# Order of three weight splits, the first gather and a conditional block in the expert stage of a fused block kernel

## The chip, the cores and the metric

The kernel runs on one core of one Trainium2 chip. The metric is device time of one execution in microseconds (us). Three runs of the kernel before took 2264.12, 2265.87 and 2269.25 us; their median is 2265.87 us. Clock rows give TensorE's granted clock as a share of its full speed.

## The reference

The reference computes two transformer-like blocks on 512 tokens of width 1024 in float32. The stage that is changed here is the mixture of experts in the middle of the first block. Cut to what matters:

```python
logits = xt @ w_router + b_router                 # 512 tokens, 32 experts
top_vals, top_idx = lax.top_k(logits, 4)          # four experts a token
weights = jax.nn.softmax(top_vals, axis=-1)
# for each expert, on the tokens that chose it:
gu = xblk @ w_gu[e] + b_gu[e]                     # 1024 -> 2048
gate, up = jnp.split(gu, 2, axis=-1)
gate = jnp.minimum(gate, 7.0)
up = jnp.clip(up, -7.0, 7.0)
act = (up + 1.0) * gate * jax.nn.sigmoid(1.702 * gate)
y[token] += weight * (act @ w_down[e] + b_down[e])   # 1024 -> 1024
```

Every expert's weights are read once: 8 MB of w_gu and 4 MB of w_down in float32. Before this stage stand a modulated norm, a gated linear attention with pooling and the router; after it a second block with Fourier mixing, attention and a recurrent layer.

## The kernel before, in words

The program is written with a planner: the code traces instructions, and a planner with a cost model of its own puts them into one fixed order for each engine. Trace order is the priority; an instruction that the model holds to be ready sooner may be put ahead of one traced earlier. `tc.issue_after(ins)` adds one constraint: what the block traces on the engine of `ins` stands behind `ins` in that engine's order. On the chip each engine then works through its own list in order and waits at semaphores.

**Precision.** Each float32 weight block is split into two parts, `whi` (the rounded part, a cast on ACT, L147) and `wlo` (the rest, a subtraction on DVE, L148), by `split`. Products are the sum of three matmuls: whi with xTh, wlo with xTh, whi with xTl.

**Weights.** `Weights.get` takes the next raw block of [128, 2048] words (1 MB). Nine raw buffers rotate; SP issues the load of a block when the split of the block nine earlier has released its buffer. Four pairs of whi and wlo rotate as well (`pair`); a split can start when TensorE has finished with the block four earlier.

**One expert** (96 slots for its tokens) is `gate_up(e)`: 8 blocks of w_gu, for each 3 x 4 matmuls into `pgu` (four PSUM banks, one buffer), then four bias matmuls (L1139); `swiglu(e)`: on DVE g (L1166) and u (L1168) read pgu, on ACT the Silu (L1167), on DVE u times g (L1169); `down(e - 1)`: two bias matmuls, then 4 blocks of w_down (called d0, d2, d4 and d6 here, after k0), for each 2 x 3 x 2 matmuls into `pd` (L1183), then y on DVE (L1186) and a scatter with addition on POOL (L1187); `turn`: transposes of the activation (`paT`, they need u) into aTh and aTl. So TensorE's stream is gate_up(e), then down(e - 1) while DVE and ACT make the activation of e, and so on for 32 experts. In gate_up the transposes of the next expert's gathered tokens (`pxT`) stand at block 5, and for every fourth expert up to 24 the tables of the next four experts (`tables`) at block 1. In expert 6 there is extra work on DVE (`vectors`).

**The start.** The normed tokens go to DRAM (`h2d`, POOL's queue). Seven blocks of w_gu have been loaded by SP; blocks 7 and 8 are put on POOL's queue right behind the last h2d write (L1201); then POOL issues the gather of expert 0's tokens (L1119). `overflows` counts the blocks beyond 96 slots into a register of every engine (L995). `overflow` is a branch (L1007): if there are further blocks, a loop computes them; with these inputs it is jumped over. In trace order it stands ahead of the first three splits of expert 0 (`held`) and of `tables(0)`. It also takes one pair of the four (`ow`).

**The end.** The scatter of expert 31 must land before the next stage (`phase_c`) reads ydr back (hr, L1750). Meanwhile phase_c prepares spectra (pG) and its first weights.

Of the kernel before, what the change touches and what calls it, by code (L numbers as in the profile page):

```python
# [9 lines left out]
F32 = mybir.dt.float32  # L10
# [5 lines left out]
OP = mybir.AluOpType  # L16
# [4 lines left out]
D = 1024  # L21
# [5 lines left out]
NE = 32  # L27
TK, XK, BK = 1, 5, 4

AH, SH, HN = 9, 7, 3  # L30
# [76 lines left out]
def bcast(ap, n, off=0, parts=128):  # L107

    return bass.AP(tensor=ap.tensor, offset=ap.offset + off, ap=[[0, parts], [1, n]])
# [33 lines left out]
def split(S, hi, lo, src):  # L143
    if S.any:
        S.nc.any.tensor_copy(hi, src)
    else:
        S.nc.scalar.copy(hi, src)  # L147
    S.nc.vector.tensor_tensor(lo, src, hi.bitcast(F32), op=OP.subtract)  # L148


def mm3(S, ps, lh, ll, rh, rl, start, stop):
# [6 lines left out]
class Weights:  # L158
# [45 lines left out]
    def get(self, view, shape):  # L204
        S = self.S
        rv = self.early.pop(0) if self.early else self.load(view, shape)
        n = int(np.prod(shape[1:]))
        hi, lo = self.pair()
        hv, lv = hi[:shape[0], :n], lo[:shape[0], :n]
        if len(shape) == 3:  # L210
            hv = hv.rearrange("p (a b) -> p a b", a=shape[1])
            lv = lv.rearrange("p (a b) -> p a b", a=shape[1])
        split(S, hv, lv, rv)
        return hv, lv
# [742 lines left out]
def tables(S, pl, bank, b):  # L957

    nc = S.nc
    es = slice(b * 4, b * 4 + 4)  # L960
    oh = pl.tile([128, NT, 4, SLOTS], BF, name="oh", tag="oh", bufs=1)
    iota = S.k[:, None, K_IOTA:K_IOTA + SLOTS].to_broadcast([128, 4, SLOTS])
    for i in range(NT):
        nc.vector.tensor_tensor(oh[:, i], iota, S.pos[:, i, es, None].to_broadcast([128, 4, SLOTS]), op=OP.is_equal)
    p = bank("ptab")
    for e in range(4):
        for i in range(NT):
            nc.tensor.matmul(p[:SLOTS, e * 6:e * 6 + 6], oh[:, i, e, :], S.V[:, i, b * 4 + e, :], start=i == 0, stop=i == NT - 1)
    sl = pl.tile([SLOTS, 4, 6], F32, name="sl", tag="sl", bufs=2)
    nc.vector.tensor_copy(sl, p[:SLOTS, 0:24].rearrange("p (e c) -> p e c", e=4))  # L970
    t = pl.tile([SLOTS, 4, 4], F32, name="tsl", tag="tsl", bufs=2)
    tok, sct = t[:, :, 0], t[:, :, 1]
    nc.vector.tensor_tensor(tok, sl[:, :, 0], sl[:, :, 1], op=OP.add)
    nc.vector.tensor_copy(S.gi[:, es], tok)

    nc.vector.scalar_tensor_tensor(sct, sl[:, :, 2], S.k[:SLOTS, K_NSLOT:K_NSLOT + 1], tok, op0=OP.mult, op1=OP.add)
    nc.vector.tensor_scalar(S.si[:, es], sct, S.k[:SLOTS, K_SLOT:K_SLOT + 1], None, op0=OP.add)
    nc.vector.tensor_tensor(sct, sl[:, :, 3], sl[:, :, 4], op=OP.add)
    nc.vector.tensor_tensor(S.wt[:, es], sct, sl[:, :, 5], op=OP.add)
# [114 lines left out]
def phase_b(S):  # L1094
    nc, tc, I = S.nc, S.tc, S.I
    mm = nc.tensor.matmul
    with ExitStack() as bx:
# [4 lines left out]
        W = Weights(S, bx, 2048, 9, "b_w", (2, 3, 0, 1, 4, 5, 8, 6, 7))  # L1102
        W.open_parts(bx, 4, "b_wp", (0, 1, 2, 3, 4, 7, 6, 5))
        pl = bx.enter_context(tc.tile_pool(name="b_pool", bufs=1, reuse_waits="tile"))
        ps = bx.enter_context(tc.tile_pool(name="b_ps", bufs=1, space=PSUM, reuse_waits="tile"))

        def bank(name):
            return ps.tile([128, 512], F32, name=name, tag="tr", bufs=2)
# [5 lines left out]
        xg, xT, aT, ac = {}, {}, {}, {}  # L1114

        def gather(e, gi=None):
            xg[e] = pl.tile([SLOTS, D], F32, name="xg", tag="xg", bufs=2)
            gi = S.gi[:, e:e + 1] if gi is None else gi
            S.gathered = nc.gpsimd.indirect_dma_start(out=xg[e], out_offset=None, in_=S.h2d,  # L1119
                                         in_offset=bass.IndirectOffsetOnAxis(ap=gi, axis=0)).ins  # L1120

        def turn(src, dst, e, name, bufs, scale=1.0):
            dst[e] = [pl.tile([128, KT, SLOTS], F32R, name=name + n, tag=name + n, bufs=bufs) for n in "hl"]
            for h in range(2):
                p = bank("p" + name)
                for k in range(4):
                    kk = h * 4 + k
                    nc.tensor.transpose(p[:, k * SLOTS:(k + 1) * SLOTS], src[:, kk * 128:(kk + 1) * 128], S.ident[:SLOTS, :SLOTS])  # L1128
                hi, lo = [t[:, h * 4:h * 4 + 4, :] for t in dst[e]]
                p = p[:, :4 * SLOTS].rearrange("p (k t) -> p k t", k=4)  # L1130
                if scale == 1.0:
                    split(S, hi, lo, p)
                else:
                    nc.scalar.mul(hi, p, scale)
                    nc.vector.scalar_tensor_tensor(lo, p, scale, hi.bitcast(F32), op0=OP.mult, op1=OP.subtract)

        def bias(p, e, c, b, start, stop):
            lhs = sel[:, b // 3, e:e + 1].to_broadcast([128, SLOTS])
            mm(p[:, c * 512:(c + 1) * 512], lhs, bt[:, b % 3 * 512:(b % 3 + 1) * 512], start=start, stop=stop)  # L1139
# [22 lines left out]
        def swiglu(e, p):  # L1162

            g = pl.tile([SLOTS, D], F32, name="g", tag="g", bufs=1)
            u = pl.tile([SLOTS, D], F32, name="u", tag="u", bufs=1)
            nc.vector.tensor_scalar(g, p[:, 0:D], 7.0, None, op0=OP.min)  # L1166
            nc.scalar.activation(g, g, AF.Silu, scale=ALPHA)  # L1167
            nc.vector.tensor_scalar(u, p[:, D:2 * D], 7.0, -7.0, op0=OP.min, op1=OP.max)  # L1168
            nc.vector.scalar_tensor_tensor(u, u, 1.0, g, op0=OP.add, op1=OP.mult)  # L1169
            return u  # L1170

        def down(e):
            p = ps.tile([SLOTS, D], F32, name="pd", tag="dn", bufs=1)
            for c in range(2):
                bias(p, e, c, 4 + c, True, False)
            ah, al = aT.pop(e)
            for k0 in range(0, KT, 2):
                wh, wl = W.get(I["w_down"][0, e, k0 * 128:(k0 + 2) * 128, :].rearrange("(k p) c -> p k c", p=128),
                               [128, 2, D])
                for k in range(2):  # L1180
                    for a, w in ((ah, wh), (ah, wl), (al, wh)):
                        for c in range(2):
                            mm(p[:, c * 512:(c + 1) * 512], a[:, k0 + k, :], w[:, k, c * 512:(c + 1) * 512],  # L1183
                               start=False, stop=k0 + k == KT - 1 and a is al)
            y = pl.tile([SLOTS, D], F32, name="y", tag="y", bufs=2)
            nc.vector.scalar_tensor_tensor(y, p, S.wt[:, e:e + 1], S.g2b, op0=OP.mult, op1=OP.mult)  # L1186
            nc.gpsimd.indirect_dma_start(out=S.ydr, out_offset=bass.IndirectOffsetOnAxis(ap=S.si[:, e:e + 1], axis=0),  # L1187
                                         in_=y, in_offset=None, compute_op=OP.add)

        sel = pl.tile([128, 2, NE], F32R, name="sel")  # L1190
        ahead = [I["w_gu"][0, e, k * 128:(k + 1) * 128, :] for e in range(2) for k in range(KT)]
# [5 lines left out]
                nc.sync.dma_start(br[64 + h:96 + h, 0:512], bgu[:, 1536:2048])  # L1197
                nc.sync.dma_start(br[64 + h:96 + h, 512:1536], bdn)
        S.ahead = W.last

        with tc.issue_after(S.h2d_last):  # L1201
            W.ahead(ahead[SH:AH], [128, 2048], nc.gpsimd)
        nc.vector.tensor_copy(sel.rearrange("p h e -> p (h e)"), S.k[:, K_SEL:K_SEL + 64])
        gather(0, S.gi0)
        with tc.issue_after(S.gathered):
            nc.gpsimd.dma_start(S.g2b, bcast(S.adr, D, off=3 * D, parts=SLOTS))
        with tc.issue_after(S.gathered):
            overflows(S, pl)
        overflow(S, pl, ps, bank, W)
        held = [W.get(I["w_gu"][0, 0, k * 128:(k + 1) * 128, :], [128, 2048]) for k in range(HN)]  # L1210
        tables(S, pl, bank, 0)
        gather(1)
        turn(xg.pop(0), xT, 0, "xT", 2)
        for e in range(NE + 1):
            if e < NE:
                between = {BK: biases} if e == 0 else {}
                if e % 4 == 0 and e // 4 + 1 < NE // 4:
                    between[TK] = lambda: tables(S, pl, bank, e // 4 + 1)
                if e + 1 < NE:
                    between[XK] = lambda: turn(xg.pop(e + 1), xT, e + 1, "xT", 2)  # L1220
                p = gate_up(e, between)
                ac[e] = swiglu(e, p)
                if e == 6:
                    vectors(S, pl, bank)
                if e + 2 < NE:
                    gather(e + 2)
            if e > 0:
                down(e - 1)
            if e < NE:
                turn(ac.pop(e), aT, e, "aT", 1, 1.0 / ALPHA)  # L1230


def turned(S, pl, bank, xT, i, xn):
# [710 lines left out]
```

## Time and profile before

| | us |
|---|---|
| runs, median (lowest to highest) | 2265.87 (2264.12 to 2269.25) |
| profiled execution, its own time | 2268.54 |
| span of its trace, first to last instruction | 2266.8 |
| mean granted clock of TensorE | 0.981 |
| TensorE busy (share of the span) | 2152.4 (95%) |
| DVE busy | 1807.6 (80%) |
| ACT busy | 1333.3 (59%) |
| POOL busy | 301.3 (13%) |

The expert stage runs from about 316 us, the first pgu matmul, to about 1515 us, the last pd matmul. Busy time of TensorE is that of pipelined matmuls; a matmul of 512 columns is shown with some 0.39 us but the next one starts 0.23 us later. "Idle before" is the idle time of an engine just ahead of an instruction, with what ended it. An engine with `q` behind its name is that engine's sequencer, which waits, branches and issues transfers.

### The profile page before, as it was taken

The page shows a single profiled execution, that of the slowest core. Times are in us where ns is not written, and L with a number is a line of the kernel's source. Part 1 is how long each engine was busy: PE and PEld are TensorE (multiplying, and loading weights), DVE is VectorE, ACT ScalarE, POOL GpSimd, SP SyncE. Part 2 cuts the span into 40 slices and gives each one's busy share as a digit, 9 for nine tenths or more (in the row PEclk, how much of TensorE's full clock was granted, in tenths as well). Part 3 has the DMA queues.
Part 4 walks back from the last instruction along what each step waited for, and adds up shares of the span by engine and source line. Part 5 has one row for each costly group of instructions (what it writes and reads, how often), then busy time and mean ns, then how long its engine had stood idle before and what let it go on. Part 6 is the DMA issues. An engine that isn't in the chain of part 4 may idle for free.

```text
span 2266.8 us, 27655 instructions
## 1 busy us (share of the span) xinstructions
PE 2152.4 (95%) x10495; PEld 1627.5 (72%) x10495; DVE 1807.6 (80%) x2020; ACT 1333.3 (59%) x1489; POOL 301.3 (13%) x157
## 2 busy tenths in 40 slices
PE   6899979999999999999999999998999999999998
PEld 4787756777766666666666666667777888877876
DVE  5669789999988989898989898976478354689885
ACT  4335356777766666666666666754455443388862
POOL 1101120010122222222222121231000000000000
PEclk9899989999999999999999999999999999999999
DMA  7664579999999999999999999966311233423222
GB/s 269 196 218 151 190 253 338 378 366 368 363 344 353 357 358 354 356 353 364 345 359 351 363 355 365 337 199 223 103 47 47 84 121 131 129 66 93 93 84 93
DMA packets 155999, 561.96 MB, mean 248 GB/s; under 512 B 12964, under 2 KB 55304, under 8 KB 123080
## 3 DMA queue, kind: packets, MB, share of 16 engines
q1 hardware_dynamic: 144832, 522.37, 62.7%
q0 software_dynamic: 9968, 36.10, 6.0%
q10 hardware_dynamic: 1064, 1.70, 0.2%
q8 instruction: 83, 1.36, 0.2%
q14 instruction: 52, 0.43, 0.1%
HBM read 534.94 MB, written 25.58 MB: 247 GB/s over the span
## 4 chain that ended last, share of the span: by engine, by line
PE 81%; DVE 10%; DMA 4%; issue 3%; ACT 2%; POOL 1%; ACTq 0%; POOLq 0%; DVEq 0%; SPq 0%
PE pgu L1156 30%; PE pd L1183 12%; DVE wlo L148 3%; PE pjf L153 3%; PE pjf L154 3%; PE pjf L155 3%; PE pop L155 2%; PE pop L153 2%; PE pop L154 2%; DVE u L1168 1%; PE pgu L1139 1%; DMA ydr<-y,si 1%; DMA raw<-in_w_ada_dram 1%; PE pxT L1128 1%; PE paT L1128 1%
## 5 line engine op out<-in xcount | busy, mean ns | idle before, releaser
L148 DVE TENSOR_TENSOR wlo<-raw,whi 128x2048 fp32r<-128x2048 f32 (+2 forms) x498 | 1001.8, 2038 | 106.1 <-ACT whi L147 83.6
L147 ACT CAST whi<-raw 128x2048 fp32r<-128x2048 f32 (+2 forms) x454 | 790.6, 1777 | 191.6 <-PE pgu L1156 87.2
L1187 POOL DMA_INDIRECT ydr<-y,si x32 | 185.1, 5783 | 809.5 <-DVE y L1186 778.0
L1156 PE MATMUL pgu<-whi,xTh 128*96 128x512 f32 x1024 | 281.6, 396 | 2.6 <-DVE u L1168 2.6
L1156 PE MATMUL pgu<-wlo,xTh 128*96 128x512 f32 x1024 | 278.7, 394 | 0.3 <-DVE wlo L148 0.3
L1156 PE MATMUL pgu<-whi,xTl 128*96 128x512 f32 x1024 | 278.5, 394 | 0.0
L1156 PEld LDWEIGHTS pgu<-wlo,xTh 128*96 128x96 f32 x1024 | 165.5, 162 | 70.9 <-DVE wlo L148 0.7
L1156 PEld LDWEIGHTS pgu<-whi,xTl 128*96 128x96 f32 x1024 | 165.4, 162 | 69.8 <-issue 0.2
L1156 PEld LDWEIGHTS pgu<-whi,xTh 128*96 128x96 f32 x1024 | 161.7, 162 | 69.9 <-issue 3.0
L1183 PE MATMUL pd<-wlo,aTh 128*96 128x512 f32 x512 | 162.4, 398 | 32.5 <-DVE wlo L148 32.5
L153 PE MATMUL pjf<-xTh,whi 128*128 128x512 f32 (+1 forms) x480 | 181.8, 379 | 1.5 <-DVE rsq L221 1.5
L155 PE MATMUL pjf<-xTh,wlo 128*128 128x512 f32 (+1 forms) x480 | 180.5, 377 | 1.9 <-DVE wlo L148 1.9
L154 PE MATMUL pjf<-xTl,whi 128*128 128x512 f32 (+1 forms) x480 | 181.0, 377 | 0.0
L1183 PE MATMUL pd<-whi,aTh 128*96 128x512 f32 x512 | 159.7, 393 | 0.0
L1183 PE MATMUL pd<-whi,aTl 128*96 128x512 f32 x512 | 159.4, 392 | 0.0
L1183 PEld LDWEIGHTS pd<-wlo,aTh 128*96 128x96 f32 x512 | 79.1, 162 | 72.3 <-DVE wlo L148 43.2
L1167 ACT ACTIVATE g<-g 96x1024 f32<-96x1024 f32 x32 | 33.9, 1061 | 137.2 <-DVE g L1166 137.2
L1183 PEld LDWEIGHTS pd<-whi,aTh 128*96 128x96 f32 x512 | 82.4, 161 | 35.3
L1183 PEld LDWEIGHTS pd<-whi,aTl 128*96 128x96 f32 x512 | 82.4, 161 | 35.4
L155 PEld LDWEIGHTS pjf<-xTh,wlo 128*128 128x128 f32 x480 | 90.3, 188 | 18.7 <-DVE wlo L148 2.3
L153 PEld LDWEIGHTS pjf<-xTh,whi 128*128 128x128 f32 x480 | 90.5, 188 | 18.1 <-ACT jkr L1509 1.4
L154 PEld LDWEIGHTS pjf<-xTl,whi 128*128 128x128 f32 x480 | 90.5, 188 | 15.8
(536 smaller groups left out, 3511.7 us busy)
## 6 DMA issues: line engine op xcount, KB each, us to landing
raw<-in_w_gu_dram SPq DMA_DIRECT2D x254, 1024.0 KB, 9.6
raw<-in_w_down_dram SPq DMA_DIRECT2D x128, 1024.0 KB, 7.2
raw<-in_w_ada_dram SPq DMA_DIRECT2D x40, 512.0 KB, 5.6
raw<-in_even_w_in_dram SPq DMA_DIRECT2D x36, 512.0 KB, 3.4
raw<-in_odd_w_in_dram SPq DMA_DIRECT2D x32, 512.0 KB, 3.8
raw<-in_even_w_out_dram SPq DMA_DIRECT2D x16, 512.0 KB, 3.1
raw<-in_odd_w_out_dram SPq DMA_DIRECT2D x16, 512.0 KB, 3.2
raw<-in_w_in_dram SPq DMA_DIRECT2D x14, 512.0 KB, 3.7
```

The costliest lines, as they stand in the source:

```text
L147: S.nc.scalar.copy(hi, src)
L148: S.nc.vector.tensor_tensor(lo, src, hi.bitcast(F32), op=OP.subtract)
L153: mm(ps, lh, rh, start=start, stop=False)
L154: mm(ps, lh, rl, start=False, stop=False)
L155: mm(ps, ll, rh, start=False, stop=stop)
L1128: nc.tensor.transpose(p[:, k * SLOTS:(k + 1) * SLOTS], src[:, kk * 128:(kk + 1) * 128], S.ident[:SLOTS, :SLOTS])
L1139: mm(p[:, c * 512:(c + 1) * 512], lhs, bt[:, b % 3 * 512:(b % 3 + 1) * 512], start=start, stop=stop)
L1156: mm(p[:, c * 512:(c + 1) * 512], a[:, k, :], w[:, c * 512:(c + 1) * 512], start=k == 0 and w is wh and a is xh, stop=False)
L1167: nc.scalar.activation(g, g, AF.Silu, scale=ALPHA)
L1168: nc.vector.tensor_scalar(u, p[:, D:2 * D], 7.0, -7.0, op0=OP.min, op1=OP.max)
L1183: mm(p[:, c * 512:(c + 1) * 512], a[:, k0 + k, :], w[:, k, c * 512:(c + 1) * 512], start=False, stop=k0 + k == KT - 1 and a is al)
L1187: nc.gpsimd.indirect_dma_start(out=S.ydr, out_offset=bass.IndirectOffsetOnAxis(ap=S.si[:, e:e + 1], axis=0), in_=y, in_offset=None, comput ...
```

## The change

`split` remembers its subtraction in `S.split_last`. In the loop over experts the splits of the down blocks d0, d2 and d4 of expert e - 1 are traced ahead of `swiglu(e)`, and swiglu's instructions on DVE are queued behind the last of them. `down` takes these three from a list and splits d6 itself; then it traces the splits of the next expert's first three w_gu blocks, and y on DVE is queued behind the last of those. At the start the two weight loads of POOL's queue go behind the first gather instead of behind the last h2d write, and `tables(0)` is traced ahead of the first three splits. The branch for further blocks is traced behind the whole loop.

```diff
@@ split
-    S.nc.vector.tensor_tensor(lo, src, hi.bitcast(F32), op=OP.subtract)
+    S.split_last = S.nc.vector.tensor_tensor(lo, src, hi.bitcast(F32), op=OP.subtract).ins
@@ down
+        def down_weights(e, k0):
+            return W.get(I["w_down"][0, e, k0 * 128:(k0 + 2) * 128, :].rearrange("(k p) c -> p k c", p=128), [128, 2, D])
-        def down(e):
+        def down(e, early):
...
             for k0 in range(0, KT, 2):
-                wh, wl = W.get(I["w_down"][0, e, k0 * 128:(k0 + 2) * 128, :].rearrange("(k p) c -> p k c", p=128),
-                               [128, 2, D])
+                wh, wl = early.pop(0) if early else down_weights(e, k0)
...
+            if e + 2 < NE:
+                held.extend(W.get(I["w_gu"][0, e + 2, k * 128:(k + 1) * 128, :], [128, 2048]) for k in range(HN))
             y = pl.tile([SLOTS, D], F32, name="y", tag="y", bufs=2)
-            nc.vector.scalar_tensor_tensor(y, p, S.wt[:, e:e + 1], S.g2b, op0=OP.mult, op1=OP.mult)
+            with tc.issue_after(S.split_last):
+                nc.vector.scalar_tensor_tensor(y, p, S.wt[:, e:e + 1], S.g2b, op0=OP.mult, op1=OP.mult)
@@ start of the stage
-        with tc.issue_after(S.h2d_last):
-            W.ahead(ahead[SH:AH], [128, 2048], nc.gpsimd)
         nc.vector.tensor_copy(sel.rearrange("p h e -> p (h e)"), S.k[:, K_SEL:K_SEL + 64])
         gather(0, S.gi0)
+        with tc.issue_after(S.gathered):
+            W.ahead(ahead[SH:AH], [128, 2048], nc.gpsimd)
...
-        overflow(S, pl, ps, bank, W)
+        tables(S, pl, bank, 0)
         held = [W.get(I["w_gu"][0, 0, k * 128:(k + 1) * 128, :], [128, 2048]) for k in range(HN)]
-        tables(S, pl, bank, 0)
@@ loop over experts
-                ac[e] = swiglu(e, p)
+                early = [down_weights(e - 1, k0) for k0 in (0, 2, 4)] if e else []
+                with tc.issue_after(S.split_last):
+                    ac[e] = swiglu(e, p)
...
+            else:
+                early = []
             if e > 0:
-                down(e - 1)
+                down(e - 1, early)
             if e < NE:
                 turn(ac.pop(e), aT, e, "aT", 1, 1.0 / ALPHA)
+        overflow(S, pl, ps, bank, W)
```

## Rows read from the trace of the kernel before

**Rows 1.** Windows of one expert: busy us (x) PE, PEld, DVE, ACT, POOL; clock; DMA share, GB/s.
```profile
408.20:444.08 35.88, 35.88 (x168) 25.48 (x167) 33.43 (x21) 25.54 (x18) 2.88 (x2) 1.00 1.00 371
444.08:480.69 36.61, 36.61 (x183) 26.19 (x183) 35.55 (x32) 25.53 (x18) 3.16 (x2) 1.00 1.01 368
891.43:929.82 38.39, 36.98 (x183) 26.08 (x183) 35.66 (x32) 24.68 (x18) 10.15 (x2) 1.00 0.97 357
1001.42:1038.88 37.46, 36.05 (x168) 25.36 (x167) 33.03 (x21) 24.89 (x18) 8.21 (x2) 1.00 0.98 357
```

**Rows 2.** Groups by line, one of pd: busy us, mean ns, idle before, releaser.
```profile
L1183 PE MATMUL pd<-wlo,aTh 128*96 128x512 f32 x512 | 162.4, 398 | 32.5 <-DVE wlo L148 32.5
```

**Rows 3.** Timeline of PE, a late expert: start us, us, what, count [idle before, releaser].
```profile
816.50 0.71 PE L1183 MATMUL pd<-wlo,aTh 128*96 128x512 f32 x2 [1.41 <-DVE wlo L148]
...
819.33 0.74 PE L1128 MATMUL paT<-cst_k,u 96*128 96x96 f32 x7
```

**Rows 4.** Timeline of DVE, the same late expert.
```profile
811.89 1.22 DVE L1166 TENSOR_SCALAR g<-pgu 96x1024 f32<-96x1024 f32 x1 [3.39 <-PE pgu L1139]
...
814.16 2.28 DVE L148 TENSOR_TENSOR wlo<-raw,whi 128x2048 fp32r<-128x2048 f32 x1
816.36 1.21 DVE L1169 SCALAR_TENSOR_TENSOR u<-u,g 96x1024 f32<-96x1024 f32 x1
```

**Rows 5.** Timeline of DVE, an early expert.
```profile
441.95 2.29 DVE L148 TENSOR_TENSOR wlo<-raw,whi 128x2048 fp32r<-128x2048 f32 x1 [0.48 <-ACT whi L147]
444.16 1.22 DVE L1166 TENSOR_SCALAR g<-pgu 96x1024 f32<-96x1024 f32 x1
...
446.43 2.28 DVE L148 TENSOR_TENSOR wlo<-raw,whi 128x2048 fp32r<-128x2048 f32 x1
448.63 1.21 DVE L1169 SCALAR_TENSOR_TENSOR u<-u,g 96x1024 f32<-96x1024 f32 x1
```

**Rows 6.** Timeline of ACT, the same early expert.
```profile
442.73 1.91 ACT L147 CAST whi<-raw 128x2048 fp32r<-128x2048 f32 x1 [0.81 <-PE pgu L1156]
...
446.92 1.92 ACT L147 CAST whi<-raw 128x2048 fp32r<-128x2048 f32 x1 [0.45 <-PE pd L1183]
```

**Rows 7.** Timeline of PE, the same early expert: the bias matmuls that end pgu.
```profile
442.53 1.09 PE L1139 MATMUL pgu<-bt,sel 128*96 128x512 f32 x4
```

**Rows 8.** Waits of SP's queue, 400 to 1480 us: us in total, times, longest.
```profile
SPq L197 <- DVE wlo L148: 868.4, 320, 7.6
```

**Rows 9.** Timeline of SP: the issue of one load.
```profile
420.85 0.37 SPq L197 DMA_DIRECT2D raw<-in_w_down_dram  x1
```

**Rows 10.** The page, DMA issues: count, KB each, median us from issue to landing.
```profile
raw<-in_w_gu_dram SPq DMA_DIRECT2D x254, 1024.0 KB, 9.6
```

**Rows 11.** Timeline of POOL, the start of the stage.
```profile
301.54 1.06 POOL L197 DMA_DIRECT2D raw<-in_w_gu_dram  x2
304.83 1.01 POOL L1119 DMA_INDIRECT xg<-h2d,gi  x1 [2.23 <-DMA h2d<-h]
```

**Rows 12.** Timeline of PE, the start of the stage.
```profile
314.39 0.58 PE L1128 MATMUL pxT<-cst_k,xg 96*128 96x96 f32 x2 [0.66 <-DMA xg<-h2d,gi]
```

**Rows 13.** Tile xg: landing of all 32 gathers.
```profile
DMA to landing us min/median/max: 8.8/10.8/13.2
```

**Rows 14.** Line 1187: landing of all 32 scatters.
```profile
DMA to landing us min/median/max: 7.0/13.5/24.0
```

**Rows 15.** Line 1007, the branch on PE's sequencer: ns min/median/max, first and last start.
```profile
L1007 PEldq COMPARE_BRANCH  x1: 6032/6032/6032, 306.2 to 306.2; - x1
```

**Rows 16.** The chain of waits at the stage's end: start us, us, what.
```profile
1521.39 6.98 DMA ydr<-y,si
1528.50 3.32 DMA hr<-ydr
```

**Rows 17.** Timeline of PE, the end of the stage.
```profile
1517.71 0.80 PE L153 MATMUL pG<-ws,whi 128*128 128x256 f32 x2 [2.26 <-ACT ws L147]
...
1533.52 0.39 PE L153 MATMUL pG<-ws,whi 128*128 128x256 f32 x1 [3.46 <-ACT spx L1404]
```

## The prediction

> **What bounds the kernel now.** The page alone does not tell: over the span TensorE is busy for 95% and DVE for 80%. The first view that does is a window per expert [rows 1]. An early expert takes 35.88 us and TensorE is busy for all 35.88 of them; one in which the next four experts' tables are made takes 36.61 us, also without a gap. A late expert takes 37.46 us, with tables 38.39 us, and in both TensorE lacks 1.41 us of being busy. The matmuls are as many (168, 183), so a late one loses 37.46 - 35.88 = 1.58 us. The second view, the groups by line, says where [rows 2]: the pd matmuls that read wlo have 32.5 us of idle time before them, all ended by DVE's wlo; at 1.41 us a time that is 23 waits, one in each of 23 late calls of down.
>
> The third view, the timeline, shows how one comes about [rows 3, 4]. DVE stands idle for 3.39 us until pgu is finished, because g is next in its order; it does g and u, and only then the split at 814.16, which ends at 816.44. TensorE has done the first down block by then and reads wlo of the second at 816.50. In an early expert [rows 5, 6] splits run until 444.24, then comes g, and one down split is left behind it (446.43). That it is the last one, d6, is read from ACT: the cast at 442.73 waited for pgu, the next, at 446.92, for pd, so that one is the next expert's first block. Early experts have d0, d2 and d4 ahead of g, late ones d0 alone. Nothing in the code differs between them; the planner's order does.
>
> **The change part by part.** *Three splits ahead of g.* No instruction is added or removed in the loop; the constraint gives every expert but the first the order of rows 5. Its price on DVE: g starts 0.54 us after the bias matmuls that end pgu (444.16 against 443.62) [rows 5, 7], where it started at once. Queued behind g are u, d6's split and u times g; TensorE has 11 us of pd to do before it needs pgu again (48 matmuls, 0.23 us apart), so 0.54 us hide there. The gain is measured by the early experts. Of the 22 late stretches from one g to the next, 18 are without tables, 18 x 1.58 = 28.4 us; 4 have them (experts 12, 16, 20, 24), 4 x (38.39 - 36.61) = 7.1 us; the 23rd wait, in the last experts, is 1.6 us. Sum 37.1 us; counted from the waits alone, 23 x 1.58 = 36.3 us. I take 36.5 us. Bounds: 0, if the order stays, and 23 x 1.78 = 41 us.
>
> What is late next: early experts keep DVE busy for 33.43 of 35.88 us, 35.55 of 36.61 with tables [rows 1], so it has 1.1 to 2.5 us to spare. SP's queue waits for raw buffers that DVE's splits release, 320 times [rows 8], so it is ahead, not behind. The load issued at 420.85 is cast at 442.73 [rows 6, 9], 21.9 us later, and such loads land in some 9.6 us [rows 10]: 12 us are left over, at 371 GB/s.
>
> [...]
>
> *y behind the next expert's three splits.* y frees pd, which the next pd bias needs. If the bias stands right ahead of the next down, some 22 us later, this costs nothing. If it stands early among the pgu matmuls, it costs up to one split, 2.3 us, an expert. I take 0: early experts run without a gap.
>
> *Gather ahead of the two loads.* POOL issues two 1 MB loads at 301.54 and the gather at 304.83, when h2d has landed [rows 11]. Expert 0's transposes start as the gather lands, 9.5 us after its issue [rows 12]. Its issue can't move, its landing can: nothing of its own queue is ahead of it any more. Gathers land in 8.8 us at best with the stage's traffic around them [rows 13], scatters of the same rows in 7.0 [rows 14]. Bounds: 0.7 us of gain (8.8) and 5.5 us (a landing in 4, the scatter's best less the reading that its addition needs, an estimate from rows 14). I take 2.5 us, by the best scatter, the nearest row with little beside it. The two loads go out some 4.3 us later, behind the gather's end of 305.84; with 12 us left over between landing and cast (above) nothing waits for them. The tables of expert 0 ahead of its first splits only change places on a DVE that waits for the gather there; 0.
>
> *The branch at the end.* At the start PE's branch took 6.03 us [rows 15], from 306.2 to 312.2, in the shadow of the gather; taking it away there gives nothing beyond the 2.5 us, and makes them possible. At the end it follows pd's last matmul, which ended at 1517.71 - 2.26 = 1515.45, and puts pG off to 1521.5, by 3.8 us [rows 17]. The chain there does not go through PE: scatter 31 takes 6.98 us, then hr is read from 1528.50 [rows 16]; and PE has a gap of 3.46 us at 1533.52 that takes up most of the 3.8. Left over 0.3 us; DVE, ACT and SP jump as well, and I take 1 us of loss. Bounds: 0 and 6.03 us, more if the next stage's preparation is held back (a rival below).
>
> **Sum.** -36.5 - 2.5 + 1 = -38 us. From the profiled execution's 2268.54 us (its span of 2266.8 and 1.7 us around it) that is 2230.5. It ran 2.67 us, 0.12%, above the median of the runs shown; from the median, 2265.87 - 38 = 2227.9, so 2228 us.
>
> **The rivals.**
>
> *The transposes of u stand too early on TensorE.* In the late order paT stands 26 matmuls into pd: the first block's 12 and two that read whi only, then the wait, then 12 more [rows 3]. There u times g ended at 817.57 [rows 4], in time for 819.33. In the new order it ends at 449.84, 6.2 us after pgu [rows 5, 7], and 26 matmuls take 26 x 0.23 = 6.0. If the planner keeps paT there, TensorE waits 0.2 us, with the refill some 0.4 (1.58 - 1.41 is the refill of a wait), 31 times, 12 us: 2240. For it: the planner's late orders have it so. Against: in early experts paT stands behind all of pd.
>
> *The other side: one more split ahead of u times g.* From the point at which u ends later than the 26th matmul, each further split ahead of it costs its 2.2 us: 8.4 against 6.0 us, with the refill 2.6 us x 31 = 80 us, so 2228 + 80 = 2308, slower than before. For it: u times g only has to stand behind d4, and a split of the next expert may go ahead of it while it waits for the Silu. Against: in both orders one split alone stood between [rows 4, 5].
>
> *The branch holds the next stage back.* If it waits for the last scatter, pG starts at 1528.4 + 6.0 instead of 1517.71, 16.7 us later, less the gap of 3.46: 13 us, so 2241. For it: the block that is jumped over scatters into ydr, and the next stage uses its space. Against: at the start the branch let PE go at 312.2, two us before a gather in flight had landed [rows 12, 15].
>
> *The transfers are the bound.* If late experts run at 357 GB/s because they must, 13.3 MB take 37.3 us, 0.2 us gained 23 times: 2265.87 - 3.7 - 1.5 = 2260.7. Against: rows 8 to 10, and early experts at 368 to 371. [...]
>
> *The change does not do what it says*: the orders stay as they are, and only start and end move: 2265.87 - 1.5 = 2264.4.
>
> **How the numbers follow.** My forecast has 0.68 (own range 2221 to 2236: the bounds of gather and branch, and 2 us either way in the loop), early transposes 0.11, a branch that holds back 0.08, transfers 0.03, no change of order 0.03, the other side 0.07. The range, 2221 to 2247, holds the first three, 0.87, less some 0.05 at its low end. A difference under 0.2%, 4.5 us, can't be told from none here. Faster by more: 0.68 + 0.11 + 0.08 + 0.03 = 0.90; within: 0.03; slower: 0.07.
>
> **What would show it.** Right: three down splits ahead of g in every expert but the first, no idle time before pd ended by wlo, windows of 35.9 us (36.6 with tables) at 368 GB/s or more up to the last expert, the gather landing some 7 us after issue, PE's branch behind pd, and hr read as soon as scatter 31 has landed. Wrong: windows that stay above 36.5 us, casts that wait for loads, idle time before paT, or hr read late.

## The result and the profile after

The changed kernel takes 2239.78 us (median of four runs, 2238.43 to 2243.24), the kernel before 2265.3 us beside it: ratio 0.9887, 95% interval 0.9869 to 0.9904, 25.5 us faster. Forecast were 38 us and 2228 us. The time lies inside the range (2221 to 2247) and outside the forecast's own (2221 to 2236). The profiled executions ran 2268.54 us before and 2238.43 us after, with spans of 2266.8 and 2236.7 us. The 30.1 us between the spans can be placed: 3.0 lie ahead of everything that was changed (the stages before run in 300.2 to 303.4 us in the fourteen traces of this study, by chance), and the other 27.1 are what is to be explained.

The loop does what it was to do. Windows of an ordinary expert, and of two of which the first has the tables (columns as in [rows 1]):

```profile
701.72:737.69 35.97, 35.97 (x168) 25.51 (x167) 33.09 (x22) 24.77 (x17) 8.24 (x2) 1.00 1.01 373
737.69:810.39 72.70, 72.70 (x350) 51.72 (x349) 68.65 (x53) 49.53 (x34) 17.24 (x4) 1.00 1.00 369
```

These are experts which took 37.46 and 38.39 + 37.46 us before [rows 1]; TensorE now has no gap. The group that had 32.5 us of idle time [rows 2] has none:

```profile
L1185 PE MATMUL pd<-wlo,aTh 128*96 128x512 f32 x512 | 159.9, 393 | 0.0
```

DVE's timeline of a late expert has the order of [rows 5] in place of that of [rows 4]: no wait ahead of g, one split between u and u times g, two behind it.

```profile
663.56 2.29 DVE L148 TENSOR_TENSOR wlo<-raw,whi 128x2048 fp32r<-128x2048 f32 x1
665.76 1.21 DVE L1166 TENSOR_SCALAR g<-pgu 96x1024 f32<-96x1024 f32 x1
666.90 1.21 DVE L1168 TENSOR_SCALAR u<-pgu 96x1024 f32<-96x1024 f32 x1
668.03 2.28 DVE L148 TENSOR_TENSOR wlo<-raw,whi 128x2048 fp32r<-128x2048 f32 x1
670.23 1.22 DVE L1169 SCALAR_TENSOR_TENSOR u<-u,g 96x1024 f32<-96x1024 f32 x1
671.36 4.49 DVE L148 TENSOR_TENSOR wlo<-raw,whi 128x2048 fp32r<-128x2048 f32 x2
```

At the start the gather is issued ahead of the two loads and lands 5.0 us later instead of 9.5 ([rows 11, 12]; POOL's timeline, and the shortest landing of tile xg):

```profile
302.03 1.29 POOL L1119 DMA_INDIRECT xg<-h2d,gi  x1 [3.51 <-DVE ox L988]
303.32 1.18 POOL L197 DMA_DIRECT2D raw<-in_w_gu_dram  x2
```

```profile
DMA to landing us min/median/max: 5.0/11.9/12.8
```

Counted from the end of the DVE instruction that makes the gather's indices (gi, L949, 303.37 before and 300.35 now), the transposes start 6.7 us behind it, 11.0 before [rows 12]. But the first matmul of pgu comes only 1.9 us earlier (11.0 behind gi for 12.9) and the second group waits for a split (TensorE's timeline):

```profile
307.06 1.54 PE L1128 MATMUL pxT<-cst_k,xg 96*128 96x96 f32 x8 [2.23 <-DMA xg<-h2d,gi]
...
311.36 2.00 PE L1156 MATMUL pgu<-whi,xTh 128*96 128x512 f32 x4
314.44 2.02 PE L1156 MATMUL pgu<-wlo,xTh 128*96 128x512 f32 x4 [1.08 <-DVE wlo L148]
```

DVE and ACT show one part of why. Expert 0's tables and xTl now stand ahead of its first split, which starts 11.8 us behind gi (2.6 before), and xTh ahead of the first cast, 8.7 us behind gi (0.7 before). TensorE stands idle for 4.1 us between pgu's first matmul and the first g, for splits, a cast and the bias table; before, it had no gap there. The other part is TensorE's clock. It is granted 0.50 up to 319.3 us before and 319.9 us now, so the earlier pgu works at it for 8.6 us instead of 3.0, some 2.8 us lost (an estimate: half of the 5.6 us; four pgu matmuls took 2.00 us there and 1.07 at 1.00, in the kernel before at 339 us). Windows, before and then changed (columns as in [rows 1]):

```profile
316.31:319.30 2.99, 2.99 (x9) 1.98 (x9) 2.04 (x7) 0.98 (x1) 0.30 (x1) 0.50 1.02 404
```

```profile
311.36:319.90 8.54, 7.46 (x19) 4.59 (x19) 8.36 (x12) 4.95 (x3) 0.00 (x0) 0.50 0.96 277
```

The first g comes 44.3 us behind gi, 40.1 before: 4.3 us lost where 2.5 were to be gained.

At the end, the branch (line 1007; count, duration in ns, first and last start):

```profile
L1007 SPq EVENT_SEMAPHORE  x9: 17/17/17, 1477.3 to 1487.5; - x9
...
L1007 SPq COMPARE_BRANCH  x1: 50/50/50, 1476.8 to 1476.8; - x1
L1007 PEldq COMPARE_BRANCH  x1: 383/383/383, 1478.7 to 1478.7; - x1
...
L1007 POOLq INC_SWDGE_SEM  x1: 1980/1980/1980, 1484.5 to 1484.5; - x1
```

TensorE jumps in 0.38 us, where the start took 6.03 [rows 15]. SP, however, is held in its nine semaphore events for 10.2 us. Four of them come some 0.02 us behind the landing of a transfer that SP itself had issued just ahead of the branch (env at 1474.07 and the three loads shown below; the trace's semaphore records have the landings at 1481.73, 1483.04, 1485.92 and 1487.22). In E2, below, SP is through at 1540.4, before POOL reaches its branch at 1540.7. So SP was held here until what it had in flight had landed, the last of it at 1487.22, and was through at 1487.5. In the kernel before its last transfers had landed 33 us ahead of the events (273.8 us for 306.6), and the nine took 0.6 us. The loads of fourier_w (fw) go out behind the events (SP's timeline) and pG waits for these (TensorE's):

```profile
1474.62 1.54 SPq L197 DMA_DIRECT2D raw<-in_even_w_in_dram  x3
1487.70 1.03 SPq L1387 DMA_DIRECT2D fw<-in_fourier_w_dram  x2
...
1489.94 2.54 SPq L1760 DMA_DIRECT2D hr<-ydr  x4
```

```profile
1481.69 0.63 PE L1185 MATMUL pd<-whi,aTl 128*96 128x512 f32 x2
1493.20 0.80 PE L153 MATMUL pG<-ws,whi 128*128 128x256 f32 x2 [10.88 <-ACT ws L147]
```

pG follows pd by 10.9 us instead of 2.3 [rows 17]. The chain of waits shows a gain beside it, scatter 31 issued 1.6 us behind pd's end where it was 5.9 [rows 16, 17], and a loss, hr's landing:

```profile
1483.91 5.97 DMA ydr<-y,si
...
1490.47 7.17 DMA hr<-ydr
```

hr is read 8.2 us behind pd's end, where it was 13.1 [rows 16, 17], and takes 7.2 us instead of 3.3 [rows 16], with the late loads beside it.

Four points divide each trace: gi, the first g, the end of the last pd matmul, the end of the span. They serve for all kernels below (us; E1 to E12 are the experiments; the ratio is to the kernel before in the same comparison, with its 95% interval):

| kernel | median | ratio | gi to first g | first g to last pd | behind |
|---|---|---|---|---|---|
| before | 2265.3 | | 40.07 | 1172.01 | 751.3 |
| changed | 2239.78 | 0.9887 [0.9869, 0.9904] | 44.33 | 1137.63 | 754.3 |
| E1 loop alone | 2227.26 | 0.9824 [0.9811, 0.9838] | 41.12 | 1132.07 | 749.8 |
| E2 start and end alone | 2294.26 | 1.0121 [1.0105, 1.0136] | 43.82 | 1189.74 | 755.6 |
| E3 branch at the start | 2225.46 | 0.9821 [0.9807, 0.9834] | 40.81 | 1132.07 | 748.1 |
| E4 splits ahead of tables | 2235.68 | 0.9860 [0.9845, 0.9875] | 40.07 | 1137.64 | 754.5 |
| E5 no branch | 2235.75 | 0.9860 [0.9845, 0.9875] | 43.86 | 1138.74 | 748.9 |
| E6 two early splits | 2227.38 | 0.9825 [0.9811, 0.9838] | 40.69 | 1132.07 | 751.3 |
| E7 one early split | 2280.07 | 1.0061 [1.0046, 1.0076] | 40.79 | 1184.25 | 750.5 |
| E8 y free | 2228.82 | 0.9833 [0.9820, 0.9847] | 40.89 | 1134.87 | 749.3 |
| E9 branch between experts | 2249.49 | 0.9923 [0.9910, 0.9937] | 48.68 | 1145.18 | 748.5 |
| E10 as E9, no branch | 2240.53 | 0.9882 [0.9867, 0.9897] | 47.91 | 1138.94 | 751.0 |
| E11 one more split | 2225.80 | 0.9819 [0.9804, 0.9834] | 39.88 | 1132.83 | 749.6 |
| E12 transposes first | 2228.60 | 0.9827 [0.9813, 0.9840] | 44.55 | 1131.90 | 748.5 |

The stretch behind the loop has the same code in all: 748.1 to 751.3 us in the eleven traces without the branch there, 754.3 to 755.6 in the three with it. Traces without it differ by up to 3.2 us there, so a single pair says little; by the means of the two groups, 749.7 and 754.8, the branch costs 5.1 us. So of the 27.1 us, the loop gave 34.4, the start lost 4.3 and the end 3.0.

### The profile page after: what moved, and what is told of

It reads as the page before. It is cut to its first block, busy times and chain, and to the rows that moved or that the text cites. A ratio compares the mean times of both kernels' runs of the same rounds, so it can differ in the third digit from the quotient of the medians.

```text
span 2236.7 us, 27602 instructions
## 1 busy us (share of the span) xinstructions
PE 2152.8 (96%) x10495; PEld 1629.9 (73%) x10495; DVE 1806.4 (81%) x2020; ACT 1324.8 (59%) x1488; POOL 319.6 (14%) x157
## 4 chain that ended last, share of the span: by engine, by line
PE 86%; DVE 7%; DMA 2%; ACT 2%; issue 2%; POOL 0%; POOLq 0%; SPq 0%; DVEq 0%; ACTq 0%
PE pgu L1156 31%; PE pd L1185 16%; PE pjf L153 3%; PE pjf L154 3%; PE pjf L155 3%; PE pop L155 3%; PE pop L153 3%; PE pop L154 3%; DVE wlo L148 2%; PE pgu L1139 1%; PE pxT L1128 1%; PE paT L1128 1%; DMA raw<-in_w_ada_dram 1%; PE pd L1139 1%; PE pw L153 1%
## 5 line engine op out<-in xcount | busy, mean ns | idle before, releaser
L1193 POOL DMA_INDIRECT ydr<-y,si x32 | 192.8, 6027 | 846.3 <-DVE y L1192 816.7
L1156 PE MATMUL pgu<-whi,xTh 128*96 128x512 f32 x1024 | 287.0, 397 | 4.0 <-DVE u L1168 3.0
L1134 ACT ACTIVATE aTh<-paT 128x384 fp32r<-128x384 f32 x64 | 28.1, 490 | 127.6 <-PE paT L1128 124.9
```

Of the source, the lines that this page charges most:

```text
L1156: mm(p[:, c * 512:(c + 1) * 512], a[:, k, :], w[:, c * 512:(c + 1) * 512], start=k == 0 and w is wh and a is xh, stop=False)
```

## The experiments

The theory after the two traces: the loop gives 34 to 37 us as forecast, and start and end lose some 4 us (the start still counted by the clock time of the first g, as 1.2) instead of gaining 1.5. The rival: the loop gives less, start and end are near nothing.

### Which part gives what: E1, E2, E3

E1 is the kernel before with the loop's edits, E2 the kernel before with those of start and end.

> The loop's part alone (three down splits ahead of g, y behind the next splits, three splits of the next expert traced in down); start and branch as in the kernel before. Theory: the loop gives what the two traces show between the first g and the last pd matmul, 1172.0 - 1137.6 = 34.4 us, and start and end together lose 4.2 us of it again: 2265.3 - 34.4 = 2231 us, some 9 us below the changed kernel's median. Rival: the loop itself gives less than the early experts promised and the start and end are near nothing (-1.5 us, as predicted): then this kernel takes some 2265.3 - 24 = 2241 us, as long as the changed one.

> The gather ahead of the two weight loads and the branch at the end alone; the loop as in the kernel before. Theory: the start loses 1.2 us (the first splits come later) and the end loses 3.0 us (SP's loads for the next stage wait behind the branch): 2265.3 + 4.2 = 2269.5 us. Rival: they bring what was predicted, -1.5 us: 2263.8 us.

E1 took 2227.26 us, 39.1 us less than before: the loop alone is worth all of the forecast and more. E2 took 2294.26 us, 27.9 us more than before, over six times the theory's loss, and 17.7 of them in the loop, of which the theory said nothing. The group of pd matmuls of E2 says what happened:

```profile
L1183 PE MATMUL pd<-wlo,aTh 128*96 128x512 f32 x512 | 164.7, 403 | 42.6 <-DVE wlo L148 42.6
```

42.6 us instead of 32.5 [rows 2]: with the branch at the end, the waits of late experts begin with expert 2's pd and not with expert 8's, the late stretches take 37.65 us where [rows 1] had 37.46, and the one with the extra work of expert 6 takes 43.02 us where it took 35.67. So the early experts owed their good order to the old start. E2 changes three things there, the places of the branch, the tables and the gather, and no run moves one of them alone with the loop as before: that it is the branch is likely and not shown. The parts don't add: -39.1 and +27.9 are -11.2, both together -25.5.

E3 is the changed kernel with the branch back at its old place:

```diff
             overflows(S, pl)
+        overflow(S, pl, ps, bank, W)
         tables(S, pl, bank, 0)
...
-        overflow(S, pl, ps, bank, W)
```

> The changed kernel with the branch back at the start, ahead of expert 0's first splits and tables; the gather stays ahead of the two loads. Theory: the 3.0 us at the end come back, since SP issues the loads of fourier_w before the last pd matmul again; the start is that of the kernel before, because TensorE's branch (6.0 us from 306.2) ends after the gather has landed, so the earlier gather is worth nothing there: 2239.8 - 3.0 - 1.2 = 2235.5 us. Rival: the end is long for another reason (scatter 31, hr's read at 7 us), and the start gains by its three earlier splits alone: 2238.5 us.

2225.46 us, 14.3 us less than the changed kernel, where the theory had 4.3 and the rival 1.3. By the table 3.5 us are gained at the start, 5.6 in the loop and 6.2 behind it. The end is as the theory had it: fw is issued at 1466.09, 7.6 us ahead of pd's end, and pG starts 2.8 us behind it:

```profile
1466.09 2.45 SPq L1387 DMA_DIRECT2D fw<-in_fourier_w_dram  x2
```

```profile
1476.44 0.79 PE L153 MATMUL pG<-ws,whi 128*128 128x256 f32 x2 [2.77 <-ACT ws L147]
```

### What the branch costs, and what its place does to the order: E4, E5

E4 queues expert 0's tables on DVE behind its first three splits, E5 leaves the call of `overflow` out:

```diff
-        tables(S, pl, bank, 0)
         held = [W.get(...) for k in range(HN)]
+        with tc.issue_after(S.split_last):
+            tables(S, pl, bank, 0)
```

> The changed kernel with expert 0's first three splits queued ahead of its tables on DVE, which also puts four casts ahead of xTh on ACT; branch at the end as changed. Theory: the late first splits (wlo at 312.1 us, 306.0 before) ate the gather's 5 us; with splits and gather both early, pgu starts near 311 us and runs without waits for splits: some 4 us less than the changed kernel, 2236 us. Rival: TensorE's lower granted clock over the first 8 us of pgu is what ate it, whatever the splits do: 2239 us, within 1 us of the changed kernel.

> The changed kernel without the conditional block at all (it is skipped on this data, so the work is the same; left out is the handling of experts with more than 96 tokens). Theory: of the 14.3 us between the changed kernel and the one with the branch at the start, what lies behind the last pd matmul (6.2 us by the two traces) is SP's loads behind the branch and goes, and what lies in start and loop (3.1 and 5.6 us) is the planner's order there, which follows from the branch not standing at the start, and stays: 2239.8 - 6.2 = 2233.6 us. Rival: the branch costs by being executed, wherever its price shows: 2225 us or less.

E4: 2235.68 us, 4.1 us less, as the theory had it; the first g is 4.3 us nearer to gi, the loop unchanged. TensorE's 4.1 us of gaps ahead of the first g are gone. The rival has a share in it: pgu starts 1.3 us later behind gi, and 3.2 us of it run at 0.50 of the clock instead of 8.6. The two are not separated here. What the prediction held to "only change places on a DVE that waits for the gather there" cost up to 4 us. E5: 2235.75 us, 4.0 us less; 5.4 us go behind the last pd, where pG now follows by 2.7 us, and nothing goes at the start or in the loop:

```profile
1487.11 0.72 PE L153 MATMUL pG<-ws,whi 128*128 128x256 f32 x2 [2.67 <-ACT ws L147]
```

So the branch costs some 4 (medians) to 6 us (traces) at the end by being carried out there; the other 9 us, at the start and in the loop, come when the branch does not stand at the start, and stay without any branch. Most of them go with the planner's other order, a part with TensorE's clock. Of the 5.6 us in the loop, 1.6 are TensorE at its lower clock: it waited 2.98 us at expert 1's first matmul and got 0.50 of its clock for the next 3.4 us; in E3 it waited 2.57 us at the same place and kept 1.00 (windows of both, columns as in [rows 1]).

```profile
347.20:350.60 3.40, 3.40 (x8) 2.23 (x9) 3.40 (x3) 2.89 (x3) 0.00 (x0) 0.50 0.75 259
```

```profile
344.10:347.60 3.50, 3.50 (x15) 2.44 (x16) 3.50 (x3) 0.79 (x2) 0.00 (x0) 1.00 1.03 410
```

The clock did not go by the length of this wait. In E2 it kept 1.00 behind 2.98 us; in the kernel before it fell to 0.50 for 3.4 us behind 2.58 us, and in E11 behind 2.57 us (window):

```profile
345.20:348.60 3.40, 3.40 (x9) 2.21 (x8) 3.40 (x5) 0.00 (x0) 0.00 (x0) 0.50 1.03 411
```

So these 1.6 us are not shown to come from the branch's place. Of the rest, 1.5 us lie in the second stretch (36.99 us for 35.48) and 1.6 in the 22 late ones, some 0.07 us each (35.96 for 35.89). Why these differ was not found.

### How the early splits work: E6, E7, E8, E11

All four start from E3. E6 and E7 change the list of early blocks:

```diff
-                early = [down_weights(e - 1, k0) for k0 in (0, 2, 4)] if e else []
+                early = [down_weights(e - 1, k0) for k0 in (0, 2)] if e else []      # E6
+                early = [down_weights(e - 1, k0) for k0 in (0,)] if e else []        # E7
```

> The kernel with the branch at the start, but two down splits instead of three traced ahead of g. Theory: two blocks are 24 matmuls or 5.5 us of TensorE work, and g, u and d4's split behind them take 4.6 us, so TensorE still finds d4 in time, and in the order written for this kernel a third split goes ahead of g anyway or d4 is in time behind it: 2225.5 us, within 2 us. Rival: three are needed, as in the early experts: a wait of some 1.4 us comes back in each of 31 experts, 2225.5 + 31 x 1.58 = 2274 us.

> The same with one down split ahead of g, the order of the late experts of the kernel before. Theory: one block is 12 matmuls or 2.8 us of TensorE work, g, u and d2's split take 4.6 us: TensorE waits 1.41 us for d2's wlo and loses 1.58 us, in some 31 experts: 2225.5 + 49 = 2274 us. Rival: the waits come from something else that moved with the early splits (y, the next expert's splits in down): 2226 us.

E6 took 2227.38 us, not to be told from E3, and the loop took the same 1132.07 us: two early splits do. E7 took 2280.07 us, 54.6 us more, and the group of [rows 2] is back to the tenth:

```profile
L1185 PE MATMUL pd<-wlo,aTh 128*96 128x512 f32 x512 | 162.7, 399 | 32.5 <-DVE wlo L148 32.5
```

The mechanism is shown: a late second split is what TensorE waits for, 23 times 1.41 us. The expectation had the count and the price wrong, and they nearly cancel: the first eight experts keep their good order, and a stretch from expert 9 on takes 38.33 us for 35.89, 2.44 us more instead of 1.58. Most of the difference is a second wait, 0.5 us in pgu, which 17 of these 22 stretches have.

E8 takes the constraint off y and the next expert's splits out of `down`:

> The kernel with the branch at the start, but y free: not queued behind a split, and the next expert's three splits not traced in down. In the order y then stands behind one split after u times g. Theory: y then waits for pd with DVE idle, some 2.6 us of its 2.8 us of idle time in an expert, so it costs nothing: 2225.5 us, within 2 us. Rival: while DVE waits for pd the next expert's splits are late and TensorE waits for them: 1 us or more in each of 31 experts, 2257 us.

2228.82 us, 3.4 us more, with overlapping runs; the loop is 2.8 us longer, mostly where the tables are made. y's place costs nothing, as forecast, and freeing it gains nothing.

E11 puts one further split, that of the next expert's first block, between u and u times g, the rival on the other side:

```diff
             nc.vector.tensor_scalar(u, p[:, D:2 * D], 7.0, -7.0, op0=OP.min, op1=OP.max)
+            more()       # d6's split, then that of the next expert's block 0
+            with tc.issue_after(S.split_last):
                 nc.vector.scalar_tensor_tensor(u, u, 1.0, g, op0=OP.add, op1=OP.mult)
```

> The kernel with the branch at the start, and d6's split and the first split of the next expert's blocks both ahead of u times g (the rival that was to cost 80 us). Theory: it costs next to nothing, because the paT transposes do not stand 26 matmuls into pd in the new order but behind all 48 of pd (11 us) and u times g ends some 8.4 us after pgu: 2225.5 us, within 3 us. Rival, as predicted: paT is due at 6.0 us and waits 2.4 us with 0.2 us of refill in each of 31 experts: 2305 us.

2225.80 us, 0.3 us more than E3, for the 80 that the rival was given. DVE has the two splits where it was to have them, and u times g ends at 1210.58 (its timeline, and below it TensorE's):

```profile
1202.70 1.21 DVE L1166 TENSOR_SCALAR g<-pgu 96x1024 f32<-96x1024 f32 x1
1203.83 1.21 DVE L1168 TENSOR_SCALAR u<-pgu 96x1024 f32<-96x1024 f32 x1
1204.96 4.48 DVE L148 TENSOR_TENSOR wlo<-raw,whi 128x2048 fp32r<-128x2048 f32 x2
1209.37 1.21 DVE L1171 SCALAR_TENSOR_TENSOR u<-u,g 96x1024 f32<-96x1024 f32 x1
```

```profile
1200.07 0.62 PE L1187 MATMUL pd<-whi,aTh 128*96 128x512 f32 x2
...
1213.00 0.82 PE L1128 MATMUL paT<-cst_k,u 96*128 96x96 f32 x8
```

The price rested on paT standing 26 matmuls into pd, 6.0 us; here it stands behind all 48 and more, 12.9 us after pd's first.

### A better place or start: E9, E10, E12

E9 and E10 put two of expert 0's splits, then its xTl, then the third split, then the tables on DVE; E9 has the branch between experts 15 and 16, E10 none.

```diff
+        held = [W.get(...) for k in range(2)]
+        with tc.issue_after(S.split_last):
+            turn(xg.pop(0), xT, 0, "xT", 2)
+        held.append(W.get(I["w_gu"][0, 0, 256:384, :], [128, 2048]))
+        with tc.issue_after(S.split_last):
+            tables(S, pl, bank, 0)
         gather(1)
...
         for e in range(NE + 1):
+            if e == 16:                                  # E9
+                overflow(S, pl, ps, bank, W)
```

> The changed kernel with two further edits: at the start two splits of expert 0, then its xTl, then the third split and only then the tables on DVE; and the branch between experts 15 and 16 instead of at the end. Theory: the branch costs where the next loads wait behind it (at the end SP was held for some 10 us and the next stage's loads came late); between two experts the loads are some 12 us ahead of the casts, so it costs under 1 us there, and with pgu starting some 3 us earlier than in the kernel with the branch at the start this takes 2225.5 - 3 + 1 = 2223.5 us, or 5.6 us more if the loop stays as in the changed kernel, 2229 us. Rival: a branch costs TensorE its 6.0 us (as at the start) or SP's 10 us wherever no other wait hides them: 2229.5 to 2234 us with the better loop.

> The same start, without the conditional block (left out: experts with more than 96 tokens). Theory: the start is limited by the gather's landing at 307 us once two splits stand ahead of xTl and the tables behind it: first pgu matmul near 310 us, against 313.3 with the branch at the start: 2225.5 - 3 = 2222.5 us, 2228 us if the loop stays as in the changed kernel (5.6 us longer). Rival: TensorE's low granted clock at the start takes it back: no earlier g of expert 0 than the 341.6 us of the kernel with the branch at the start.

Both missed: 2249.49 and 2240.53 us, with 48.7 and 47.9 us from gi to the first g. The start got worse because ACT's order was not held: xTh stood ahead of the first cast, and ACT waited for it, 9.0 us in E9 and 9.2 in E10. Tables made late also make the gather of expert 1 late, for which TensorE waits in the middle of expert 0 (E10):

```profile
337.02 1.51 PE L1128 MATMUL pxT<-cst_k,xg 96*128 96x96 f32 x8 [4.66 <-DMA xg<-h2d,gi]
```

With the same start, the branch between experts costs 9.0 us by the medians, and 6.2 us of loop by the traces: the stretch that holds it takes 44.04 us instead of 36.0, and E10's first stretch is 2.4 us longer than E9's. TensorE waits once (E9):

```profile
904.08 1.14 PE L1156 MATMUL pgu<-whi,xTh 128*96 128x512 f32 x2 [6.54 <-DVEq L1007]
```

The wait is for DVE, not for SP or a load: the event on DVE's skipped path comes at 903.9, when y and aTl of the expert ahead are done, and the next expert's work is not placed ahead of the branch. The rival had the size, 6 to 10 us, and not the cause: TensorE's own jump took 0.46 us here. What this branch cost between experts was what was not placed across it, 6.54 us of waiting on TensorE.

E12 is E3 with the transposes traced ahead of the tables, and the tables queued behind xTl. In E3 TensorE stands idle for 10.42 us ahead of the transposes, which are behind a table matmul:

```profile
310.83 0.24 PE L968 MATMUL ptab<-V,oh 128*96 128x6 bf16 x1 [10.42 <-DVE oh L964]
310.93 0.56 PE L1128 MATMUL pxT<-cst_k,xg 96*128 96x96 f32 x2
...
313.30 2.00 PE L1156 MATMUL pgu<-whi,xTh 128*96 128x512 f32 x4
```

> The kernel with the branch at the start, with expert 0's transposes and xTl ahead of its tables (traced first, tables queued behind xTl on DVE). Theory: there TensorE is through its branch at 308.4 us and the gather lands at 307.9 us, but the transposes stand behind the first table matmul, which waits for DVE's oh until 310.8; with the tables behind, pgu starts some 2 us earlier than 313.3 and the rest follows: 2223.5 us. Rival: the tables then come later, expert 1's gather with them, and TensorE waits for its landing in the middle of expert 0 (4.7 us where no branch stood at the start): no gain, 2225 to 2228 us.

2228.60 us; the rival's account was right, its time 0.6 us short. pgu starts 1.5 us nearer to gi, but expert 1's gather is issued 20.5 us behind gi instead of 15.6, and TensorE waits for it and then works at 0.50 of its clock up to 337.5 us (timeline, then a window of most of that stretch, columns as in [rows 1]); the first g is 3.7 us later:

```profile
332.06 0.55 PE L1128 MATMUL pxT<-cst_k,xg 96*128 96x96 f32 x2 [3.27 <-DMA xg<-h2d,gi]
```

```profile
332.10:336.60 4.50, 4.50 (x15) 3.25 (x16) 0.19 (x2) 0.53 (x1) 0.00 (x0) 0.50 1.01 401
```

E3 beats both kernels of the case, by 14.3 us and by 40.9; the runs of E1, E6, E8, E11 and, by 0.05 us, E12 overlap with its own.

## Why the prediction was right, and where it was wrong

**Three splits ahead of g: right.** Forecast -36.5 us, measured alone -39.1 (E1). The windows are those of the early experts, the waits are gone. Of the 39.9 us of the loop by E1's trace, 1.7 lie between the first g and the second (29.34 to 27.62 us) and are the clock's: TensorE waited 2.58 and 2.57 us there, and the clock fell to 0.50 in the kernel before and kept 1.00 in E1. The 22 late stretches give 36.2 us (35.5 forecast) and what follows the last g 3.2 (1.6 forecast); the eight stretches between lose 1.2.

**y: right** (E8). **Late next: right.** An expert now moves 369 to 373 GB/s in windows that had 357, so the transfers were not the bound. The 13.3 MB of an expert in the rival are 371 GB/s times 35.88 us [rows 1]; they were moved in windows of 35.97 us (373 GB/s) and not in 37.3.

**Gather: the landing right, its worth not shown.** It lands 5.0 us after issue (bounds 4 to 8.8, taken 7; the 4 was an estimate, and no run shows what the scatter's reading takes). With the branch at the start it is worth 1.8 us by the medians of E1 and E3, whose runs overlap, and 0.3 us by the first g: there the gather lands at 307.9 us, but TensorE's table matmul, ahead of the transposes, waits for DVE until 310.83. That wait was not named.

**The failed step: the branch at the end, +1 us.** It cost 14.3 us (changed kernel against E3), and failed in two ways.
- *The engine.* "The chain there does not go through PE" was worked out on TensorE's jump alone, and "DVE, ACT and SP jump as well" was given a fraction of a microsecond. SP's jump itself took 0.05 us, but SP then waited for its own transfers in flight, and the loads of the next stage behind the branch went out 5.4 us behind pd's end instead of 7.6 ahead. That cost 5.4 us (E5) to 6.2 (E3) by single traces. The rival "the branch holds the next stage back" had the effect but another cause (that it waits for the last scatter) and 13 us; hr was not held back.
- *The order.* "Taking it away there gives nothing beyond the 2.5 us" and "only change places on a DVE that waits for the gather there" took the planner's order at the start as given. DVE did not wait there in the kernel before: it did splits from 305.96 to 312.66 us and the tables from 312.88. With the branch there three splits and casts filled the time ahead of it; without it the tables and xTh went first. That is 3.5 us at the start (E4 gives 4.3 back) and 5.6 us in the loop, in both with a share of TensorE's lower clock. The early experts, from which the gain was read, also owed their order to the old start: without it, and with the loop unconstrained, they are late (E2). The rival "the change does not do what it says", 2264.4 us, would have been 2294.

**Rivals.** paT stands behind pd, as in the early experts. The other side (2308) was a price without its ground: E11 puts its split there and pays 0.3 us.

So 2228 us was, by chance, the time of E1, the loop's part by itself; the 12 us missed are the branch's place. That 2239.78 us lies inside the range is luck in part: the range reached up to 2247 for two rivals, at 2240 and 2241 us. The one, early transposes, did not happen, and the other happened by another cause.

## What to carry to other kernels

The conditional block was a line across all five engines here: its branch (L1007) stood in the queue of each, and in E9 TensorE waited 6.54 us for DVE to pass it. To price a new place, list on each queue, SP's among them, what stands right behind it, what is still in flight ahead of it, and what the scheduler had put ahead of it at the old place. When a good order is found by chance in part of a loop, ask what made it good there before taking that thing away; here the constraint in the loop was worth 39 us with the branch at the start and 54 with it at the end. Moving the gather ahead paid only up to the next wait (with the branch at the start it landed at 307.9 us and TensorE waited until 310.83), so name that wait, with its time, for every engine the data goes through.

## What the runs showed of the hardware that was not expected

- TensorE was granted 0.50 up to 317 to 321 us in all fourteen traces (319.3 in the kernel before, 319.9 in the changed one), wherever between 311.4 and 316.3 us pgu started. The earlier start of the changed kernel bought time at the lower clock: 3.0 us of pgu ran at it in the kernel before, 8.6 us in the changed one.
- Behind the same wait, with TensorE at 1.00 ahead of it, the clock went both ways: 2.57 to 2.58 us left it at 1.00 in E1, E3, E6, E7 and E8 and were followed by 3.4 us at 0.50 in the kernel before and in E11; 2.98 us left it at 1.00 in E2 and were followed by 3.4 us at 0.50 in the changed kernel.
- The same branch took TensorE's sequencer 6.03 us at 306 us [rows 15], 4.73 us at 303.7 us (E3), 0.46 us at 895 us (E9) and 0.38 us at 1478.7 us (changed kernel); on SP it took 50 and on DVE 72 ns in these four traces. On SP of the changed kernel the skipped path's semaphore events took 10.2 us, not the branch; four of them came some 0.02 us behind the landing of SP's own transfers.
- The first gather landed in 4.6 to 5.6 us with no load of its queue right ahead of it (ten traces; 5.0 in the changed kernel, 5.5 in E3), and behind two 1 MB loads in 9.2 (E1) and 9.5 us (the kernel before) [rows 11, 12].
